# Softmax folded, low halves of 50 weight tiles made by adding transfers, q and k copies issued by ACT, and the conv norm's sums ordered ahead of q of heads 6 and 7

## The chip, the cores and the metric

The kernel runs on one core of a Trainium2 chip. The metric is the device time of one execution in microseconds (us). PE is the matmul engine, PEld its weight loads, DVE the vector engine, ACT the scalar engine, POOL GpSimd, and SP the engine that issues most transfers. Each engine does its instructions in the order in which they stand, and waits on semaphores for the others.

## The reference

Two blocks, one after the other, on 528 tokens (16 meta tokens and 512) of 1024 channels, all in float32. The change lies in the first:

```
n = rms(h); z = n @ w_in                       # q, k, v, glu, g_att, g_conv
s = (q * 64**-0.5) @ k, for 8 heads x 2 maps, chunk-causal mask
p = softmax(s);  a = p[0] - lam * p[1];  o = a @ v
y_att = rms(o) * 0.2;  u = glu_a * sigmoid(glu_b)
u = causal_dwconv(u, 31 taps);  u = silu(layernorm(u));  y_conv = u @ w_conv_out
m = sigmoid(g_att) * y_att + sigmoid(g_conv) * y_conv;  h = h + m @ w_out
h = h + ffn(h)                                 # gated, 2816 wide, 3-tap convs
```

The second block has two layers of a gated short conv and an 8-head retention.

## The kernel before

Every weight matrix is cut into tiles of 128x1024 float32 (512 KB), 300 of them, in the order of the list `order` (lines 78 to 121): 16 for the glu, then for each pair of heads two v tiles, and for each head a q, a k and a g_att tile, and for heads 0 to 4 a g_conv tile; then the rest of g_att and g_conv, w_conv_out, w_out, the FFN and the second block. Products are made to float32 precision from two float32r halves each: `proj` (line 150) does 24 matmuls, 8 of high weight with high x, 8 of low weight with high x, 8 of high weight with low x. So each weight tile must be split: `prep` (line 126) loads it to wraw, ACT casts it to the high half wh (line 138), and DVE subtracts to get the low half wl (line 139). Four tiles of each half are kept, so a tile's buffers come free when the tile four before it has been used.

The attention stage (lines 466 to 594) goes over 8 heads. Each head's q and k go from PSUM to qf (line 488), ql, kf and kl, and four transfers each copy them between the two halves of the partitions, to qh (line 493) and kk (line 506); POOL issues these. Then five query tiles t of scores s (PE), maximum mx (DVE), exp (ACT, with the scale 0.125 and the bias -0.125 mx), the difference a (DVE), its transposes tr (PE), their copy aTA or aTB (ACT), the products po with v, and pss, the sum of squares over a head. The PSUM tiles of the projections come from a pool of three (mmA, tag mm); tr, po and pss share one slot.

The conv of 31 taps (`conv`, lines 392 to 410: 240 DVE steps on line 405 and the running sum lnacc) is handed to the scheduler at head 5 with the lowest priority: it fills the room that DVE has left. The norm of the conv comes in two parts: `norm_1` (line 414) sums over channels (matmul lnm), subtracts the mean and adds up squares (acc_ln), and `norm_2` (line 424) sums those (matmul lnv), takes root and reciprocal (rs_ln) and applies silu. The call `later(steps, by)` (line 183) moves steps back in priority by so many. norm_1 stands in head 6 behind g_att with 300, norm_2 in head 7 with 0. The order of instructions on each engine is made by a scheduler from these priorities. After the heads come the products yc with w_conv_out, together with rb, which spreads the heads' scales, and then w_out (wo).

Of the kernel before, what the change touches and what calls it, by code (L numbers as in the profile page):

```python
# [13 lines left out]
AF = mybir.ActivationFunctionType  # L14
ALU = mybir.AluOpType
AX = mybir.AxisListType
# [3 lines left out]
D = 1024  # L20
# [18 lines left out]
N2, GCL, SP, LATE = 0, 0, 0, 2  # L39
CH, CB, N1, RB = 5, 20000, 300, 300  # L40
KB = 1
PSF = (4, 3, 1)
GC_EARLY = 5

PAR = {}
# [18 lines left out]
def kernel(ctx, tc, hT, par, pos, decay, w1, w2, out):  # L64
# [9 lines left out]
    def fv(ap):  # L74
        return ap.bitcast(F32)
# [50 lines left out]
    def prep():  # L126
        if state["next"] >= len(order):
            return
        src, idx = order[state["next"]]
        i = state["next"]  # L130
        state["next"] += 1
        src = src[idx]
        n = src.shape[1]
        raw = wpool.tile([P, D], F32, tag="wraw", bufs=2, name=f"wraw{i}")[:, :n]
        nc.sync.dma_start(raw, src)
        wl = wpool.tile([P, D], F32R, tag="wl", name=f"wl{i}")
        wh = wpool.tile([P, D], F32R, tag="wh", name=f"wh{i}")
        S.copy(wh[:, :n], raw)  # L138
        V.tensor_tensor(wl[:, :n], raw, fv(wh[:, :n]), ALU.subtract)  # L139
        ready.append((wh, wl))  # L140
# [272 lines left out]
    def norm_1():  # L413
        mu = npool.tile([P, T1], F32, tag="nrs", name="lnmu")
        for i, (c0, cn) in enumerate(C514):
            ps = mmA(f"lnm{i}")[:, :cn]
            PE.matmul(ps, lhsT=ones, rhs=ln["sum"][:, c0:c0 + cn], start=True, stop=True)
            S.activation(mu[:, c0:c0 + cn], ps, AF.Copy, scale=1.0 / D)
        ss = ln["ss"] = SumSq("ln")
        for k in range(NK):  # L420
            V.tensor_tensor(y[k], y[k], mu[:, :TQ], ALU.subtract)
            ss.add(y[k], 0, TQ)

    def norm_2():
        ss = ln["ss"]
        rs = npool.tile([P, T1], F32, tag="nrs", name="rs_ln")
        for i, (c0, cn) in enumerate(C514):
            ps = mmA(f"lnv{i}")[:, :cn]
            rstd(rs[:, c0:c0 + cn], ss.total(ps, c0, cn), D, epsc[:, 1:2])
        for k in range(NK):  # L430
            V.tensor_tensor(y[k], y[k], rs[:, :TQ], ALU.mult)
            S.activation(y[k], y[k], AF.Silu, bias=pc("conv_ln_b", k), scale=pc("conv_ln_w", k))
# [33 lines left out]
    for h in range(HEADS):  # L466
# [3 lines left out]
        if h % 2 == 0:  # L470
            wa, wb = getw(), getw()
            for tb in range(5):
                m = P if tb < 4 else META
                ps = mmA(f"v{h}_{tb}")[:m, :256]
                for p in range(3):
                    for k in range(NK):
                        w = (wa, wb)[k // 4][0 if p != 1 else 1][:, (k % 4) * 256:(k % 4 + 1) * 256]
                        x = (xh if p != 2 else xl)[k][:, tb * P:tb * P + m]
                        PE.matmul(ps, lhsT=x, rhs=w, start=p == 0 and k == 0, stop=p == 2 and k == NK - 1)  # L479
                S.copy(vt[(h // 2) % 2][:m, tb, :], ps)  # L480

        w = getw()
        qh = ap2.tile([P, 2, TQ + 2], F32R, tag="qh", bufs=1, name=f"qh{h}")
        for i, (c0, cn) in enumerate(C514):
            ps = mmA(f"q{h}_{i}")[:, :cn]
            proj(ps, w, xh, xl, TQ0 + c0, cn)
            c = slice(c0, c0 + cn)
            S.copy(qf[:, c], ps)
            for m in range(2):
                V.tensor_tensor(ql[MAP[m], m, c], ps[MAP[m]], fv(qf[MAP[m], c]), ALU.subtract)  # L490
        for m in range(2):
            for r in range(2):
                nc.gpsimd.dma_start(fv(qh[64 * r:64 * r + 64, m, :]), fv(qf[64 * m:64 * m + 64, :]))

# [9 lines left out]
        for m in range(2):  # L504
            for r in range(2):
                nc.gpsimd.dma_start(fv(kk[64 * r:64 * r + 64, m, :]), fv((kf, kl)[m ^ r][64 * m:64 * m + 64, :]))
        tg = None
# [4 lines left out]
        if h == HEADS - 1:  # L512
            att_rstd(("kf", "kl"))
            tg = g_att(h)
            later(norm_2, N2)
            for n in range(GC_EARLY, NK):
# [4 lines left out]
        if h == CH:  # L521
            later(conv, CB)
        if h == 6:
            later(norm_1, N1)
        v_ = vt[(h // 2) % 2]
# [3 lines left out]
        for t, (q0, qn, nkey) in enumerate(QT):  # L529
# [3 lines left out]
            if t < 4:  # L533
                ps = psS.tile([P, 2, 512], F32, tag="ps", name=f"s{h}_{t}")
                nw = nkey
                for m in range(2):
# [5 lines left out]
                    pm.append(ps[:qn, m, :nkey])  # L542
                V.tensor_reduce(mx[:qn], ps[:qn, :, :nkey], AX.X, ALU.max)
            else:
                for m in range(2):
# [5 lines left out]
                    pm.append(ps[:qn, 248:248 + T1])  # L551
                    V.tensor_reduce(mx[:qn, m:m + 1], pm[m], AX.X, ALU.max)
            V.tensor_scalar(mx[:qn], mx[:qn], -0.125, None, ALU.mult)
            sm = ap2.tile([P, 2], F32, tag="sm", name=f"sm{h}_{t}")
            pt = []
            for m in range(2):
                p_ = at[t] if m == 0 else ap2.tile([P, T1], F32, tag="p1", name=f"p1_{h}_{t}")
                S.activation(p_[:qn, :nkey], pm[m], AF.Exp, bias=mx[:qn, m:m + 1], scale=0.125,
                             accum_out=sm[:qn, m:m + 1])
                pt.append(p_)  # L560
# [511 lines left out]
```

## Time and profile before

| | us |
|---|---|
| three runs | 1880.42, 1882.37, 1882.59 |
| median | 1882.37 |
| the profiled execution | 1883.03 |
| its span, first to last instruction | 1881.2 |
| PE busy in the span | 1852.5 |
| DVE busy | 1311.3 |
| ACT busy | 836.1 |

Stages of the profiled execution: the glu to about 108 us, the heads to about 460, beside them yc from about 418 to 486, wo to 533, the FFN to about 900, then the second block. A busy PE is not a PE at its peak, since matmuls are pipelined and their ends are modelled; so matmuls are counted beside the busy time.

### The profile page before, as it was taken

The page shows a single profiled execution, that of the slowest core. Times are in us where ns is not written, and L with a number is a line of the kernel's source. Part 1 is how long each engine was busy: PE and PEld are TensorE (multiplying, and loading weights), DVE is VectorE, ACT ScalarE, POOL GpSimd, SP SyncE. Part 2 cuts the span into 40 slices and gives each one's busy share as a digit, 9 for nine tenths or more (in the row PEclk, how much of TensorE's full clock was granted, in tenths as well). Part 3 has the DMA queues.
Part 4 walks back from the last instruction along what each step waited for, and adds up shares of the span by engine and source line. Part 5 has one row for each costly group of instructions (what it writes and reads, how often), then busy time and mean ns, then how long its engine had stood idle before and what let it go on. Part 6 is the DMA issues. An engine that isn't in the chain of part 4 may idle for free.

```text
span 1881.2 us, 29256 instructions
## 1 busy us (share of the span) xinstructions
PE 1852.5 (98%) x11802; PEld 1685.7 (90%) x11802; DVE 1311.3 (70%) x2147; ACT 836.1 (44%) x1473; POOL 76.6 (4%) x123
## 2 busy tenths in 40 slices
PE   8999999999999999999999999999999999999997
PEld 7999999988999999988988888888899888888887
DVE  8999999876688777634588776454277877745424
ACT  7234455673445444433356553222355555422222
POOL 3000011000000000000000000000020000000000
PEclk9999999999999999999999999999999999999999
DMA  4332323222332222232323222222213222222221
GB/s 153 101 113 91 102 87 118 89 70 68 113 107 91 96 96 91 85 104 93 99 75 107 79 91 90 100 101 91 100 68 101 95 92 93 79 101 92 99 101 56
DMA packets 53047, 177.79 MB, mean 95 GB/s; under 512 B 6640, under 2 KB 10736, under 8 KB 52912
## 3 DMA queue, kind: packets, MB, share of 16 engines
q1 hardware_dynamic: 47696, 160.80, 24.8%
q0 software_dynamic: 5072, 15.12, 2.9%
q8 instruction: 93, 1.52, 0.3%
q14 instruction: 42, 0.34, 0.1%
q10 hardware_dynamic: 144, 0.00, 0.0%
HBM read 165.25 MB, written 2.10 MB: 89 GB/s over the span
## 4 chain that ended last, share of the span: by engine, by line
PE 96%; ACT 2%; DVE 1%; DMA 0%; issue 0%; POOL 0%; SPq 0%; DVEq 0%; ACTq 0%
PE up L157 13%; PE w L157 9%; PE dn L157 6%; PE rz L157 5%; PE cb L157 5%; PE cc L157 5%; PE cx L157 5%; PE cz L157 5%; PE rv L812 5%; PE rq L157 5%; PE rk L157 5%; PE v L479 3%; PE gc L157 3%; PE yc L157 3%; PE wo L157 2%; PE q L157 2%
## 5 line engine op out<-in xcount | busy, mean ns | idle before, releaser
L138 ACT CAST wh<-wraw 128x1024 fp32r<-128x1024 f32 (+1 forms) x300 | 313.3, 1045 | 490.3 <-PE dn L157 66.8
L139 DVE TENSOR_TENSOR wl<-wraw,wh 128x1024 fp32r<-128x1024 f32 (+1 forms) x300 | 364.4, 1215 | 189.2 <-ACT wh L138 188.6
L157 PE MATMUL up<-xhome,wh 128*128 128x258 f32 x1408 | 183.7, 283 | 0.0
L157 PEld LDWEIGHTS up<-xhome,wh 128*128 128x128 f32 x1408 | 175.3, 190 | 0.1
L405 DVE SCALAR_TENSOR_TENSOR y<-u,pr,y 128x514 f32<-128x514 f32 x240 | 170.2, 743 | 0.3
L157 PE MATMUL up<-xhome,wl 128*128 128x258 f32 x704 | 97.9, 281 | 0.0
L157 PEld LDWEIGHTS up<-xhome,wl 128*128 128x128 f32 x704 | 89.7, 189 | 0.0
L725 DVE SCALAR_TENSOR_TENSOR cv<-cg,pr,cv 128x256 f32<-128x256 f32 x176 | 83.7, 479 | 7.9 <-ACT cv L722 6.5
L722 ACT ACTIVATE cv<-cg,pr 128x256 f32<-128x256 f32 x88 | 52.7, 599 | 63.3 <-DVE cg L719 63.3
L812 PE MATMUL rv<-wh,xhome 128*128 128x256 f32 x512 | 75.5, 286 | 0.0
L157 PE MATMUL rq<-xhome,wh 128*128 128x512 f32 (+1 forms) x288 | 70.1, 373 | 1.3 <-ACT xhome L238 1.3
L812 PEld LDWEIGHTS rv<-wh,xhome 128*128 128x128 f32 x512 | 67.9, 191 | 1.7 <-issue 0.5
L157 PE MATMUL rk<-xhome,wh 128*128 128x512 f32 (+1 forms) x288 | 68.5, 368 | 0.0
L157 PE MATMUL rz<-xhome,wh 128*128 128x512 f32 x256 | 65.9, 391 | 0.0
L157 PE MATMUL w<-mh,wh 128*128 128x512 f32 (+1 forms) x320 | 65.7, 348 | 0.0
L157 PE MATMUL w<-mh,wl 128*128 128x512 f32 (+1 forms) x320 | 65.4, 347 | 0.0
L157 PE MATMUL cx<-xhome,wh 128*128 128x512 f32 x256 | 64.0, 390 | 0.0
L157 PE MATMUL cc<-xhome,wh 128*128 128x512 f32 x256 | 63.7, 390 | 0.0
L157 PE MATMUL cb<-xhome,wh 128*128 128x512 f32 x256 | 63.7, 389 | 0.0
L895 DVE RECIPROCAL rsq<-rsq 128x512 f32<-128x512 f32 x16 | 53.6, 3350 | 14.0 <-ACT rsq L894 14.0
L157 PE MATMUL cz<-xhome,wh 128*128 128x512 f32 x256 | 63.3, 389 | 0.0
L157 PE MATMUL w<-ml,wh 128*128 128x512 f32 (+1 forms) x300 | 62.4, 348 | 0.0
(379 smaller groups left out, 4000.1 us busy)
## 6 DMA issues: line engine op xcount, KB each, us to landing
wraw<-w_in SPq DMA_DIRECT2D x160, 512.0 KB, 3.2
wraw<-w_up SPq DMA_DIRECT2D x44, 512.0 KB, 3.2
wraw<-w_out SPq DMA_DIRECT2D x40, 512.0 KB, 3.2
wraw<-w_v SPq DMA_DIRECT2D x24, 512.0 KB, 3.2
wraw<-w_down SPq DMA_DIRECT2D x16, 512.0 KB, 3.2
qh<-qf POOLq DMA_DIRECT2D x32, 129.0 KB, 2.7
wraw<-w_conv_out SPq DMA_DIRECT2D x8, 512.0 KB, 3.2
dc<-dec POOLq DMA_DIRECT2D x16, 256.0 KB, 3.1
```

What stands on the lines that cost most here:

```text
L138: S.copy(wh[:, :n], raw)
L139: V.tensor_tensor(wl[:, :n], raw, fv(wh[:, :n]), ALU.subtract)
L157: PE.matmul(ps, lhsT=a[:, ks(k)], rhs=b[k][:, t0:t0 + n], start=first and i == 0, stop=last and i == len(steps) - 1)
L405: V.scalar_tensor_tensor(ys[i][:, :TQ], src, wj, ys[i][:, :TQ], ALU.mult, ALU.add)
L479: PE.matmul(ps, lhsT=x, rhs=w, start=p == 0 and k == 0, stop=p == 2 and k == NK - 1)
L722: S.activation(t, g[:, 0:256], AF.Identity, scale=pr[:, o:o + 1], bias=pc("ffn_dw_b", f))
L725: V.scalar_tensor_tensor(t, g[:, k:k + 256], pr[:, o:o + 1], t, ALU.mult, ALU.add)
L812: PE.matmul(ps, lhsT=xx, rhs=w, start=p == 0 and k == 0, stop=p == 2 and k == NK - 1)
L895: V.reciprocal(rr, rr)
```

## The change

Four parts.

1. Softmax: the scale 0.125 goes into the copy of q (qf and ql), the maximum is taken with its sign turned, and the multiplication of mx and the scale of exp go.
2. Low halves of weight tiles 6 to 55: in place of DVE's subtraction, ACT writes minus the rounded weight to wl, and POOL issues a transfer that reads the weight from memory again and adds it to wl where it lies.
3. The eight copies of q and k per head are issued by ACT in place of POOL.
4. norm_1 and norm_2 are called at the start of heads 6 and 7, ahead of q, with a priority raised by 300; the q matmuls of these heads are held behind the matmul of the sum just made.

```diff
@@ -37,10 +37,11 @@
 BY = (0, 0)
 LB = 0
 N2, GCL, SP, LATE = 0, 0, 0, 2
-CH, CB, N1, RB = 5, 20000, 300, 300
+CH, CB, N1, RB = 5, 20000, -300, 300
 KB = 1
 PSF = (4, 3, 1)
 GC_EARLY = 5
+ADDED = (6, 56)
 
 PAR = {}
 _off = 0
@@ -132,11 +133,18 @@
         src = src[idx]
         n = src.shape[1]
         raw = wpool.tile([P, D], F32, tag="wraw", bufs=2, name=f"wraw{i}")[:, :n]
-        nc.sync.dma_start(raw, src)
         wl = wpool.tile([P, D], F32R, tag="wl", name=f"wl{i}")
         wh = wpool.tile([P, D], F32R, tag="wh", name=f"wh{i}")
-        S.copy(wh[:, :n], raw)
-        V.tensor_tensor(wl[:, :n], raw, fv(wh[:, :n]), ALU.subtract)
+        if ADDED[0] <= i < ADDED[1]:
+
+            nc.sync.dma_start(raw, src)
+            S.copy(wh[:, :n], raw)
+            S.activation(wl[:, :n], raw, AF.Copy, scale=-1.0)
+            nc.gpsimd.dma_start(wl[:, :n], src, accum_op=ALU.add)
+        else:
+            nc.sync.dma_start(raw, src)
+            S.copy(wh[:, :n], raw)
+            V.tensor_tensor(wl[:, :n], raw, fv(wh[:, :n]), ALU.subtract)
         ready.append((wh, wl))
 
     def getw():
@@ -414,7 +422,7 @@
         mu = npool.tile([P, T1], F32, tag="nrs", name="lnmu")
         for i, (c0, cn) in enumerate(C514):
             ps = mmA(f"lnm{i}")[:, :cn]
-            PE.matmul(ps, lhsT=ones, rhs=ln["sum"][:, c0:c0 + cn], start=True, stop=True)
+            ln["mm"] = PE.matmul(ps, lhsT=ones, rhs=ln["sum"][:, c0:c0 + cn], start=True, stop=True)
             S.activation(mu[:, c0:c0 + cn], ps, AF.Copy, scale=1.0 / D)
         ss = ln["ss"] = SumSq("ln")
         for k in range(NK):
@@ -426,7 +434,8 @@
         rs = npool.tile([P, T1], F32, tag="nrs", name="rs_ln")
         for i, (c0, cn) in enumerate(C514):
             ps = mmA(f"lnv{i}")[:, :cn]
-            rstd(rs[:, c0:c0 + cn], ss.total(ps, c0, cn), D, epsc[:, 1:2])
+            ln["mm"] = PE.matmul(ps, lhsT=ones, rhs=ss.acc[:, c0:c0 + cn], start=True, stop=True)
+            rstd(rs[:, c0:c0 + cn], ps, D, epsc[:, 1:2])
         for k in range(NK):
             V.tensor_tensor(y[k], y[k], rs[:, :TQ], ALU.mult)
             S.activation(y[k], y[k], AF.Silu, bias=pc("conv_ln_b", k), scale=pc("conv_ln_w", k))
@@ -478,19 +487,24 @@
                         x = (xh if p != 2 else xl)[k][:, tb * P:tb * P + m]
                         PE.matmul(ps, lhsT=x, rhs=w, start=p == 0 and k == 0, stop=p == 2 and k == NK - 1)
                 S.copy(vt[(h // 2) % 2][:m, tb, :], ps)
+        if h == 6:
+            later(norm_1, N1)
+        if h == 6 + 1:
+            later(norm_2, N1)
 
         w = getw()
         qh = ap2.tile([P, 2, TQ + 2], F32R, tag="qh", bufs=1, name=f"qh{h}")
         for i, (c0, cn) in enumerate(C514):
             ps = mmA(f"q{h}_{i}")[:, :cn]
-            proj(ps, w, xh, xl, TQ0 + c0, cn)
+            with tc.issue_after(ln["mm"].ins) if h in (6, 6 + 1) else ExitStack():
+                proj(ps, w, xh, xl, TQ0 + c0, cn)
             c = slice(c0, c0 + cn)
-            S.copy(qf[:, c], ps)
+            S.activation(qf[:, c], ps, AF.Copy, scale=0.125)
             for m in range(2):
-                V.tensor_tensor(ql[MAP[m], m, c], ps[MAP[m]], fv(qf[MAP[m], c]), ALU.subtract)
+                V.scalar_tensor_tensor(ql[MAP[m], m, c], ps[MAP[m]], 0.125, fv(qf[MAP[m], c]), ALU.mult, ALU.subtract)
         for m in range(2):
             for r in range(2):
-                nc.gpsimd.dma_start(fv(qh[64 * r:64 * r + 64, m, :]), fv(qf[64 * m:64 * m + 64, :]))
+                nc.scalar.dma_start(fv(qh[64 * r:64 * r + 64, m, :]), fv(qf[64 * m:64 * m + 64, :]))
 
         w = getw()
         kk = ap2.tile([P, 2, T1], F32R, tag="kk", bufs=KB, name=f"kk{h}")
@@ -503,7 +517,7 @@
             split(ps, kf[:, c], kl[:, c])
         for m in range(2):
             for r in range(2):
-                nc.gpsimd.dma_start(fv(kk[64 * r:64 * r + 64, m, :]), fv((kf, kl)[m ^ r][64 * m:64 * m + 64, :]))
+                nc.scalar.dma_start(fv(kk[64 * r:64 * r + 64, m, :]), fv((kf, kl)[m ^ r][64 * m:64 * m + 64, :]))
         tg = None
         if h < HEADS - 1:
             tg = g_att(h)
@@ -512,7 +526,6 @@
         if h == HEADS - 1:
             att_rstd(("kf", "kl"))
             tg = g_att(h)
-            later(norm_2, N2)
             for n in range(GC_EARLY, NK):
                 later(lambda: g_conv(n), GCL)
             rs7 = npool.tile([P, T1], F32, tag="nrs", name="rs7")[:, :TQ]
@@ -520,8 +533,6 @@
             later(lambda: [split(y[k], uh[k][:, :TQ], ul[k][:, :TQ]) for k in range(NK)], SP)
         if h == CH:
             later(conv, CB)
-        if h == 6:
-            later(norm_1, N1)
         v_ = vt[(h // 2) % 2]
         aTA = ap2.tile([P, 2, 194], F32, tag="aTA", name=f"aTA{h}")
         aTB = ap2.tile([P, 5, 320], F32, tag="aTB", name=f"aTB{h}")
@@ -540,7 +551,7 @@
                     PE.matmul(ps[:qn, m, nkey - 64:nkey], lhsT=hid, rhs=negrow, start=False, stop=False)
                     PE.matmul(ps[:qn, m, :nw], lhsT=ql[:, m, q0:q0 + qn], rhs=kk[:, m, :nw], start=False, stop=True)
                     pm.append(ps[:qn, m, :nkey])
-                V.tensor_reduce(mx[:qn], ps[:qn, :, :nkey], AX.X, ALU.max)
+                V.tensor_reduce(mx[:qn], ps[:qn, :, :nkey], AX.X, ALU.max, negate=True)
             else:
                 for m in range(2):
                     ps = psS.tile([P, 1024], F32, tag="ps", name=f"s{h}_{t}_{m}")
@@ -549,13 +560,12 @@
                         PE.matmul(ps[:66, o:o + cn], lhsT=qh[:, m, q0:q0 + 66], rhs=kk[:, m, c0:c0 + cn], start=True, stop=False)
                         PE.matmul(ps[:66, o:o + cn], lhsT=ql[:, m, q0:q0 + 66], rhs=kk[:, m, c0:c0 + cn], start=False, stop=True)
                     pm.append(ps[:qn, 248:248 + T1])
-                    V.tensor_reduce(mx[:qn, m:m + 1], pm[m], AX.X, ALU.max)
-            V.tensor_scalar(mx[:qn], mx[:qn], -0.125, None, ALU.mult)
+                    V.tensor_reduce(mx[:qn, m:m + 1], pm[m], AX.X, ALU.max, negate=True)
             sm = ap2.tile([P, 2], F32, tag="sm", name=f"sm{h}_{t}")
             pt = []
             for m in range(2):
                 p_ = at[t] if m == 0 else ap2.tile([P, T1], F32, tag="p1", name=f"p1_{h}_{t}")
-                S.activation(p_[:qn, :nkey], pm[m], AF.Exp, bias=mx[:qn, m:m + 1], scale=0.125,
+                S.activation(p_[:qn, :nkey], pm[m], AF.Exp, bias=mx[:qn, m:m + 1],
                              accum_out=sm[:qn, m:m + 1])
                 pt.append(p_)
             V.reciprocal(sm[:qn], sm[:qn])
```

The matmuls are the same 11,696 of the program's order, and SP's list of loads is the same. From wo on, the orders of all engines are the same but for numbers. The order moves in three places that matter.

The first is PE where lnv stands, the sum of squares of the conv's norm (ga is g_att, gc g_conv, s scores, po and pss the end of a head). Before:

```order
L587 MATMUL pss_0_4313<-osq_0_4310,ones 128x194
L157 MATMUL ga_1_5016<-xhome,wh_4607 128x256 x4
L210 MATMUL lnv_5043<-acc_ln,ones 128x258
L580 MATMUL po_194_4316<-aTB_4187,v_1292 128x320 x3
L580 MATMUL po_194_4316<-aTB_4187,v_1292 128x192
L580 MATMUL po_194_4316<-aTB_4187,v_1292 128x64
L210 MATMUL lnv_5047<-acc_ln,ones 128x256
L157 MATMUL gc_0_5074<-xhome,wh_4846 128x258 x8
L157 MATMUL gc_0_5074<-xhome,wl_4845 128x258 x8
L157 MATMUL gc_0_5074<-xhome,wh_4846 128x258 x8
```

After:

```order
L165 MATMUL ga_1_4692<-xhome,wh_4349 128x256 x2
L437 MATMUL lnv_4856<-acc_ln,ones 128x258
L165 MATMUL ga_1_4692<-xhome,wh_4349 128x256 x6
L165 MATMUL ga_1_4692<-xhome,wl_4348 128x256 x8
L165 MATMUL ga_1_4692<-xhome,wh_4349 128x256 x4
L579 MATMUL tr_3_4285<-ident,a_1330 128x128 x4
L165 MATMUL ga_1_4692<-xhome,wh_4349 128x256 x3
L437 MATMUL lnv_4860<-acc_ln,ones 128x256
L165 MATMUL ga_1_4692<-xhome,wh_4349 128x256
L548 MATMUL s_0_4721<-kk_4597,qh_4529 66x80
```

The two lnv matmuls moved from g_att of head 7, where po and the next projection followed at once, into g_att of head 6, with 18 matmuls of g_att, a tr group of 4 and 3 more of g_att between the two.

The second is PE at the transposes tr of head 7, beside the products yc. Before:

```order
L615 MATMUL rb_1_5541<-rstd_sl_3186,sel 128x256
L569 MATMUL tr_0_5281<-ident,a_1311 128x66
L569 MATMUL tr_1_5302<-ident,a_1313 128x128 x2
L569 MATMUL tr_2_5324<-ident,a_1315 128x128 x3
L569 MATMUL tr_3_5347<-ident,a_1317 128x128 x4
L157 MATMUL yc_0_5552<-xhome,wh_5188 128x258 x8
L157 MATMUL yc_0_5552<-xhome,wl_5187 128x258 x8
L157 MATMUL yc_0_5552<-xhome,wh_5188 128x258 x8
L157 MATMUL yc_1_5578<-xhome,wh_5188 128x256 x2
L569 MATMUL tr_4_5375<-ident,a_1319 128x66 x5
L157 MATMUL yc_1_5578<-xhome,wh_5188 128x256 x6
```

After:

```order
L625 MATMUL rb_0_5478<-rstd_sl_3199,sel 128x258
L579 MATMUL tr_0_5295<-ident,a_1324 128x66
L625 MATMUL rb_1_5483<-rstd_sh_3198,sel 128x256
L625 MATMUL rb_1_5483<-rstd_sl_3199,sel 128x256
L165 MATMUL yc_0_5494<-xhome,wh_5143 128x258 x8
L165 MATMUL yc_0_5494<-xhome,wl_5142 128x258 x8
L165 MATMUL yc_0_5494<-xhome,wh_5143 128x258 x8
L165 MATMUL yc_1_5520<-xhome,wh_5143 128x256 x2
L579 MATMUL tr_1_5315<-ident,a_1326 128x128 x2
L165 MATMUL yc_1_5520<-xhome,wh_5143 128x256 x6
L165 MATMUL yc_1_5520<-xhome,wl_5142 128x256 x8
L165 MATMUL yc_1_5520<-xhome,wh_5143 128x256 x8
```

Four groups of tr that stood in one row are now apart, with a half of yc or more between each two.

The third is ACT behind the last q copy qf of head 4 (wh is the high half of a weight tile, wl the low one, aTA and aTB copies of transposes, tga the tanh of g_att). Before:

```order
L488 CAST qf<-q_1_3370 128x256
L138 CAST wh_3405<-wraw_3402 128x1024
L161 CAST kf_3409<-k_0_3411 128x256
L558 ACTIVATE a_1319,sm_4_3149<-s_4_0_3136,mx_4_3135 64x528
L558 ACTIVATE p_3_4_3151,sm_4_3149<-s_4_1_3142,mx_4_3135 64x528
L589 COPY ssq_1323<-pss_194_2788 1x320
L161 CAST kf_3409<-k_1_3438 128x272
L138 CAST wh_3472<-wraw_3469 128x1024
L572 COPY aTA_3043<-tr_0_3063 128x66
```

After:

```order
L502 ACTIVATE qf<-q_1_3386 128x256
L141 CAST wh_3420<-wraw_3418 128x1024
L507 DMA qh_3357<-qf 64x516 x3
L582 COPY aTA_3061<-tr_0_3080 128x66
L507 DMA qh_3357<-qf 64x516
L169 CAST kf_3426<-k_0_3428 128x256
L142 ACTIVATE wl_3487<-wraw_3486 128x1024
L169 CAST kf_3426<-k_1_3455 128x272
L141 CAST wh_3488<-wraw_3486 128x1024
L582 COPY aTA_3061<-tr_1_3100 128x2x128
L520 DMA kk_3425<-kf_3426 64x528
L520 DMA kk_3425<-kl_3427 64x528 x2
```

Among the copies that empty PSUM (qf, kf, aTA) now stand the wl copies and the issues of qh and kk. POOL's order has 50 issues of wl where the 64 issues of qh and kk were.

## Rows read from the trace of the kernel before

**Rows 1.** The page's first part: busy us (share of the span) xinstructions.

```profile
PE 1852.5 (98%) x11802; PEld 1685.7 (90%) x11802; DVE 1311.3 (70%) x2147; ACT 836.1 (44%) x1473; POOL 76.6 (4%) x123
```

**Rows 2.** Busy time by 50 us stretches, 300 to 450; the first line names the columns.

```profile
core 0: us, PE busy (x) PEld busy (x) DVE busy (x) ACT busy (x) POOL busy (x), PEclk, DMA share, GB/s
300.00:350.00 50.00, 50.00 (x412) 48.70 (x411) 46.49 (x91) 30.58 (x78) 4.07 (x8) 1.00 0.26 86
350.00:400.00 50.00, 47.01 (x347) 44.33 (x345) 38.30 (x76) 31.89 (x75) 8.16 (x16) 0.97 0.35 107
400.00:450.00 50.00, 46.99 (x348) 43.75 (x347) 31.59 (x65) 34.11 (x71) 0.00 (x0) 0.97 0.16 54
```

**Rows 3.** The same by 10 us stretches, same columns.

```profile
390.00:400.00 10.00, 8.24 (x47) 7.17 (x45) 8.74 (x12) 7.00 (x12) 0.97 (x2) 0.83 0.37 117
...
430.00:440.00 10.00, 8.55 (x65) 7.85 (x63) 5.56 (x12) 6.26 (x12) 0.00 (x0) 1.00 0.16 54
440.00:450.00 10.00, 9.16 (x63) 8.87 (x64) 5.58 (x10) 2.38 (x6) 0.00 (x0) 0.83 0.14 52
```

**Rows 4.** Waits of PE, 100 to 500 us: us in total, times, longest.

```profile
PE tr L569 <- ACT aTA L572: 1.7, 2, 1.3
PE po L580 <- ACT ssq L589: 1.2, 2, 0.6
PE lnv L210 <- ACT rs_ln L222: 1.2, 1, 1.2
PE yc L157 <- DVE tgc L607: 1.2, 1, 1.2
PE k L157 <- DVE ql L490: 1.1, 2, 0.7
PE gc L157 <- ACT rs_ln L222: 0.6, 1, 0.6
PE tr L569 <- ACT aTB L572: 0.6, 1, 0.6
```

**Rows 5.** PE in order of time: start us, us, operation, [idle before <-releaser].

```profile
362.77 1.08 PE L417 MATMUL lnm<-lnacc,ones 128*128 128x258 f32 x4
...
418.28 3.82 PE L157 MATMUL yc<-xhome,wh 128*128 128x258 f32 x15
```

**Rows 6.** Groups by line and shape, 50 to 400 us: busy, mean ns | idle before.

```profile
L405 DVE SCALAR_TENSOR_TENSOR y<-u,pr,y 128x514 f32<-128x514 f32 x237 | 168.2, 743 | 0.3
L139 DVE TENSOR_TENSOR wl<-wraw,wh 128x1024 fp32r<-128x1024 f32 x49 | 59.7, 1219 | 12.2 <-ACT wh L138 12.0
L138 ACT CAST wh<-wraw 128x1024 fp32r<-128x1024 f32 x48 | 50.3, 1048 | 16.2 <-PE gv L157 13.2 <-PE v L479 3.1
...
L493 POOL DMA_DIRECT2D qh<-qf x32 | 16.5, 526 | 320.4 <-ACT qf L488 136.6 <-issue 58.1 <-ACT p L563 32.9
```

**Rows 7.** DVE in order of time: last sum of conv, last sum of squares.

```profile
344.46 0.69 DVE L409 TENSOR_TENSOR lnacc<-lnacc,y 128x514 f32<-128x514 f32 x1
...
380.69 0.69 DVE L206 TENSOR_TENSOR acc_ln<-acc_ln,sq_ln 128x514 f32<-128x514 f32 x1
```

**Rows 8.** DMA issues on the page: KB each, median us to landing.

```profile
wraw<-w_in SPq DMA_DIRECT2D x160, 512.0 KB, 3.2
```

**Rows 9.** Issue instructions on SP and ACT: ns min/median/max, first and last start.

```profile
L135 SPq DMA_DIRECT2D wraw<-w_in x21: 327/328/332, 107.7 to 283.4; - x21
...
L166 ACTq DMA_DIRECT2D pr<-par x1: 442/442/442, 0.7 to 0.7; - x1
```

**Rows 10.** Table loads of ACT, 50 to 400 us, columns as in rows 6.

```profile
L222 ACT ACT_TABLE_LOAD x2 | 2.6, 1283 | 0.0
```

## The prediction

> **What bounds the kernel now.** I read the page's first part, then tables of stretches, then the waits of PE, then single instructions. The page [rows 1] shows PE busy 1852.5 us of 1881.2: all that any change of order can win is in the 28.7 us left, and in stretches where PE runs slowly without a gap. DVE has 70% and ACT 44% over the whole span, but this is an average over stages. The table of 50 us stretches [rows 2] shows the stage that the change touches: from 300 to 350 us PE has no gap (412 matmuls, so 0.121 us each) while DVE is busy 46.5 of 50; from 350 to 450 us PE loses 3.0 us in each stretch, and its granted clock has a mean of 0.97. The 10 us table [rows 3] finds the places: 390 to 400 and 430 to 450. In two of these stretches the clock has a mean of 0.83, which is a time at the lower level of 1.2 GHz: 0.17 of 10 us, so 1.7 us of work is lost each time, and both times PE had just stood idle. The waits of PE between 100 and 500 us [rows 4] name what it stood for, 7.6 us in all.
>
> I sort these losses into three. **A**, the norm of the conv: lnv 1.2, gc 0.6, one of the two po waits (0.6) and the longer k wait (0.7), 3.1 us, and the first clock loss, 1.7: **4.8 us**. **B**, the transposes of the last head: tr 1.7 and 0.6, the other po wait 0.6, 2.9 us, and the second clock loss, 1.7: **4.6 us**. **C**, yc for DVE, 1.2 us. A loss that no gap shows: the first 15 yc matmuls took 3.82 us [rows 5] where 15 x 0.121 is 1.8, so 2.0 us more. The ceiling is 7.6 + 3.4 + 2.0 = 13.0 us.
>
> Why A is there: the sum of the conv comes last of a long list on DVE. The 240 conv steps cost 743 ns each [rows 6], DVE does them in the room that the rest leaves, and the last sum starts at 344.46 us [rows 7]. Then lnm starts at 362.77 [rows 5], the squares are summed until 381.4 [rows 7], and lnv, which stands behind the last g_att on PE, meets a slot of PSUM that its own square root still holds.
>
> **The change, part by part.**
>
> *Low halves by adding transfers.* 50 DVE subtractions of 1219 ns go [rows 6]: 61 us of DVE work before 400 us. Nothing on PE waited for these directly; the gain is that the conv ends earlier, by up to 61 us, at about 284 us. In their place stand 50 ACT copies, which I cost like the 128x1024 cast beside them at 1048 ns [rows 6]: 52 us of ACT. Then come 50 POOL issues, for which the nearest row is the 526 ns of the q copies [rows 6], and 50 transfers that read the weight again, 512 KB each, for which the nearest row is 3.2 us to landing [rows 8]. No row shows a transfer that adds. I bound it from 3.2 us below to three times that, 9.6 us, above, and take 5. The tightest cover is the weight tile of g_att behind a pair of v tiles: its buffer comes free when v ends, and PE wants its low half 96 matmuls of q and k and 8 of its own later, 104 x 0.121 = 12.6 us. Three ACT copies (3.1), the issue (0.5) and 5 us make 8.7: hidden, cost 0. It would cost something from a landing of 9.0 us up, so the upper end costs 0.6 us at each of the four such places (heads 0, 2, 4 and 6), 2.4 us.
>
> *Copies of q and k issued by ACT.* 64 issues leave POOL, where they cost nobody anything, and come to ACT. The rows give 327 ns for an issue on SP and 442 for the only one on ACT [rows 9]: 21 to 28 us of ACT between 120 and 400 us. Each also makes ACT wait in its order, for DVE's kl or for the score matmuls that still read the old copy; behind it stand the copies that empty PSUM. POOL must be free of them, or they would stand behind adding transfers that wait for their copy. Together: 48 casts in 350 us [rows 6] are 6.9 per 50 us, so the new copies add 7.2; 64 issues over some 270 us add 3.9 to 5.2. ACT's 30.6 to 34.1 of 50 [rows 2] becomes 42 to 47, before the overlaps that busy time counts twice. This is the price of the change. Below, it is 0: ACT is under 100%, and with three PSUM tiles PE can be two groups of 24 matmuls (5.8 us) ahead. Above, each of the 16 groups of four issues holds PE for 1 us: 16. I take 2 us, near the lower end: ACT at 30.6 to 34.1 of 50 already stands beside a PE with no gap from 300 to 350.
>
> *Softmax folded.* 40 small DVE multiplications go, 32 subtractions take a scale as well, the scale moves to the q copy. All of it is DVE work in the stage where DVE gains room: 0.
>
> *The norm ordered earlier.* On PE, lnm now stands behind v of heads 6 and 7, before q of head 6, and lnv within g_att of head 6, before q of head 7. If conv ended late, PE would now be held in front of all of q; but conv ends some 50 us before, so that wait is 0. From lnm to the last sum took 18.6 us before [rows 5, 7]. Between them PE now has 130 large matmuls, 15.7 us, and about 2 us of small ones; DVE no longer has three subtractions of 1.2 us there, so I cost it 0, at most 2. The two square roots are now split by a tanh on ACT, which needs two more table loads of 1283 ns [rows 10]: 2.6 us of ACT, inside the sum above. The second lnv waits for a root that starts 25 matmuls (3 us) earlier. So A goes in full: **-4.8**.
>
> *The tail.* The transposes of head 7 stood in one row on PE, each waiting for the copy of the one before; now some 24 yc matmuls (2.9 us) stand between them. In that time ACT must do an exp, a table load, a root and the copy, about as much. I let 1.0 us of B stay: **-3.6**. C and the slow first yc stay; nothing there changed.
>
> Sum: -4.8 - 3.6 + 2.0 = -6.4 us. The profiled execution took 1883.03 us (span 1881.2 and 1.8 around it), 0.66 above the median of the three runs, 1882.37. So 1876.6 for a profiled run, **1876.0 us** against the median. Its own range is 1873 to 1880.
>
> **A rule against the change.** The 64 POOL issues before the change took a mean of 526 ns while DVE was 93% busy with the conv [rows 2, 6]; no stretched issue shows. The Trainium skill, in SBUF — State Buffer, section SBUF: two separate sides, warns of a "DVE blocks DMA" trap: a transfer issued on GpSimd can't get its descriptors written while DVE holds the shared ports in certain fast modes, and it names 620 ns that became 3100. By that figure each adding transfer would come about 2.5 us later, an estimate, which the 12.6 us would still cover. The trace speaks against it here, since the conv ran beside all those issues.
>
> **Rivals.**
>
> 1. *ACT becomes the bound* (slower). The place is q and k of every head: four issues in a row, 1.3 to 1.8 us, some of them waiting, ahead of the copies that empty PSUM. For it: ACT at up to 47 of 50 in its own order. Against it: PE had no gap beside ACT at 30.6. It decides from 0.53 us per group (8.4 / 16). At 0.8 us it costs 12.8: 1882.4 - 8.4 + 12.8 = 1886.8 us.
>
> 2. *The stall only moves.* The waits of A and B are of ACT's latency as much as of the conv's lateness: table loads and roots still stand between lnv and q, and between the last exps and tr. Then A is saved, B and its clock loss stay: -4.8 + 2 = -2.8, 1879.6 us. For it: ACT is fuller than before. Against it: the orders below the diff, where other matmuls stand in the gaps.
>
> 3. *Low halves come late.* As above, if a transfer that adds lands in 12 us or more: 3 us at each of four v pairs, 12 us, and a further clock loss: -6.4 + 12 + 1.7 = +7.3, 1889.7 us. Were it slower than a weight tile's pace, 48 tiles in 350 us or 7.3 us each, it would be tens of us more. For it: no row shows such a transfer, and the starved descriptors above would lengthen it. Against it: DMA is 0.16 to 0.35 busy [rows 2], so there is room for twice the bytes.
>
> That the change doesn't do what it says is excluded by the order of its instructions.
>
> **Chances.** The forecast's case 0.55, rival 1 0.17, rival 2 0.18, rival 3 0.10. A measurement of this kernel can tell about 0.2%, 3.8 us, so faster means under 1878.6 and slower over 1886.1. Forecast's case: 0.52 faster, 0.03 same. Rival 2: 0.06 faster, 0.11 same, 0.01 slower. Rival 1: 0.03, 0.05, 0.09. Rival 3: 0.02, 0.02, 0.06. Sum: 0.63 faster, 0.21 same, 0.16 slower. The range runs from the ceiling (1882.4 - 13.0 = 1869.4) to just past rival 1: 1869 to 1887; what is left out is rival 3's worse half and rival 1's.
>
> **What the profile after would show.** Right: the last conv step near 285 us, DVE under 40 of 50 from 300 on; PE with no lnv or gc wait, no clock below full around 390, tr waits under 1 us together; ACT 40 or more of 50 between 150 and 400; adding transfers landing in under 9 us. Wrong: PE waits for ACT (qf, kf, tga) spread over 130 to 380 us say rival 1; PE waits for DMA at the ninth matmul of a tile say rival 3; a tr wait and a clock of 0.83 near 440 again say rival 2.

## The result, and the profile after

The changed kernel takes 1898.59 us (median of four runs, 1896.26 to 1902.51) where the kernel before takes 1882.34: a ratio of 1.0094, interval 1.0078 to 1.011. It is slower by 16 us; the forecast was 6 us faster. The profiled execution took 1896.26 us, span 1894.3, so 13.1 us of span are to be accounted for.

The page of the changed kernel (first part; queues with packets, MB and share of 16 engines' span; issues with KB each and median us to landing):

```profile
PE 1856.1 (98%) x11802; PEld 1688.7 (89%) x11802; DVE 1254.9 (66%) x2057; ACT 887.7 (47%) x1525; POOL 87.1 (5%) x109
...
q1 hardware_dynamic: 47696, 160.80, 24.5%
q0 software_dynamic: 9200, 32.78, 8.9%
...
wl<-w_in POOLq DMA_DIRECT2D x42, 512.0 KB, 7.8
...
```

DVE has 56 us less work than before [rows 1], as it should, and ACT 52 more. What PE lost stands in the table of 50 us stretches, columns as in [rows 2]:

```profile
100.00:150.00 50.00, 47.31 (x398) 46.40 (x396) 44.93 (x89) 20.69 (x32) 6.05 (x7) 1.00 0.78 192
150.00:200.00 50.00, 47.00 (x367) 46.42 (x368) 42.52 (x86) 30.24 (x77) 4.32 (x5) 0.93 0.57 135
...
300.00:350.00 50.00, 47.48 (x389) 46.26 (x388) 20.68 (x44) 35.10 (x81) 5.18 (x6) 1.00 0.73 177
350.00:400.00 50.00, 46.69 (x350) 44.14 (x349) 28.03 (x53) 38.49 (x70) 4.32 (x5) 0.93 0.54 127
400.00:450.00 50.00, 48.85 (x369) 45.77 (x368) 26.35 (x57) 37.09 (x85) 1.73 (x2) 1.00 0.40 106
...
sum 400.00, PE 383.31 PEld 369.95 DVE 278.77 ACT 239.48 POOL 33.95; mean PE 47.91 PEld 46.24 DVE 34.85 ACT 29.93 POOL 4.24
```

The same eight stretches from 100 to 500 us of the kernel before:

```profile
sum 400.00, PE 392.34 PEld 379.66 DVE 342.01 ACT 207.44 POOL 35.03; mean PE 49.04 PEld 47.46 DVE 42.75 ACT 25.93 POOL 4.38
```

PE has 16.7 us of gaps in 400 where it had 7.7: 9.0 more. The clock is at a mean of 0.93 in two stretches (0.07 x 50 = 3.5 us each, 7.0), where it was at 0.97 in two (3.0): 4.0 more. Together 13.0 of the 13.1 us. By place, gaps and clock together (the stretches are of equal time, not of equal work: by 350 us the changed kernel is some 15 us behind):

| stretch, us | before | after | |
|---|---|---|---|
| 100 to 350 | 0.4 | 15.0 | +14.6, forecast at most +2.0, for ACT's issues |
| 350 to 400 (place A) | 4.5 | 6.8 | +2.3, forecast -4.8 |
| 400 to 500 (B and C) | 5.7 | 1.9 | -3.8, forecast -3.6 |

What PE waited for from 100 to 500 us, as in [rows 4]:

```profile
PE s L548 <- DMA kk<-kl: 5.0, 3, 2.4
PE s L548 <- DMA wraw<-w_in: 2.5, 1, 2.5
PE lnv L437 <- ACT rs_ln L230: 2.4, 1, 2.4
PE s L548 <- DMA wraw<-w_v: 1.7, 1, 1.7
PE s L548 <- DMA kk<-kf: 1.2, 1, 1.2
PE tr L579 <- ACT aTA L582: 1.2, 3, 0.7
PE tr L579 <- ACT ssq L599: 1.2, 2, 0.8
```

The first scores of a head (s) now wait for the copies of k and for DMA, 10.4 us in all, a wait that the kernel before doesn't have. A score reads no weight tile: where a weight load is named, a copy of k landed just behind it (in the first head the load at 148.8 us and the first copy of kl at 149.1, for a score that starts at 149.43). No row is a projection that waits for a low half. The adding transfers hurt, but not where they land: the transfers beside them come late. The issues between 100 and 400 us of the changed kernel (count, KB each, median us to landing):

```profile
q0 software_dynamic: 5376, 19.53, 36.7%
...
wl<-w_in POOLq DMA_DIRECT2D x30, 512.0 KB, 8.0
wraw<-w_in SPq DMA_DIRECT2D x30, 512.0 KB, 7.2
...
kk<-kf ACTq DMA_DIRECT2D x14, 132.0 KB, 6.1
kk<-kl ACTq DMA_DIRECT2D x14, 132.0 KB, 7.5
```

and of the kernel before:

```profile
q0 software_dynamic: 3072, 8.56, 10.8%
...
wraw<-w_in SPq DMA_DIRECT2D x30, 512.0 KB, 3.2
...
kk<-kf POOLq DMA_DIRECT2D x16, 132.0 KB, 2.9
kk<-kl POOLq DMA_DIRECT2D x16, 132.0 KB, 3.1
```

Every transfer shown takes twice as long or more: a weight load 7.2 us for 3.2, a copy of k 6.1 to 7.5 for 2.9 to 3.1. The first head shows how this reaches PE (in order of time: start us, us, operation, [idle before <-releaser]):

```profile
137.23 1.28 ACTq L520 DMA_DIRECT2D kk<-kf  x2
...
138.64 2.97 ACTq L520 DMA_DIRECT2D kk<-kl  x2
...
148.89 1.06 ACT L142 ACTIVATE wl<-wraw 128x1024 fp32r<-128x1024 f32 x1 [3.30 <-DMA wraw<-w_in]
...
149.43 0.23 PE L548 MATMUL s<-kk,qh 128*66 128x80 f32 x1 [2.46 <-DMA wraw<-w_in]
...
151.75 0.30 PE L548 MATMUL s<-kk,qh 128*66 128x80 f32 x1 [1.98 <-DMA kk<-kl]
```

The issue of two copies of kl holds ACT for 2.97 us; they land 10.5 and 11.4 us after their issues began, and PE waits twice for them. ACT's wl copy waits for a weight load, too. Then the clock falls. Ten-us stretches:

```profile
140.00:150.00 10.00, 7.32 (x62) 7.02 (x60) 7.34 (x12) 4.58 (x7) 0.86 (x1) 1.00 1.04 263
150.00:160.00 10.00, 8.25 (x50) 8.28 (x51) 5.76 (x13) 3.92 (x12) 0.86 (x1) 0.66 0.60 144
...
450.00:460.00 10.00, 9.33 (x77) 9.23 (x78) 9.58 (x18) 6.44 (x12) 0.00 (x0) 1.00 0.16 55
460.00:470.00 10.00, 10.00 (x87) 10.00 (x87) 5.88 (x12) 2.29 (x4) 0.00 (x0) 1.00 0.30 105
```

From 140 to 150 us the DMA engines have a share of 1.04: full by this measure, where the 50 us mean reads 0.78. The mean clock of 0.66 behind the two waits, part of the stretch at the 1.2 GHz level, is 0.34 x 10 = 3.4 us of work lost. The last two rows are place B, where the transposes of head 7 now stand (450.7 to 464.7 us): full clock, where before it was 0.83 [rows 3].

### The profile page after: what moved, and what is told of

Its sections match the earlier page's. It is cut to its first block, busy times and chain, and to the rows that moved or that the text cites. A ratio compares the mean times of both kernels' runs of the same rounds, so it can differ in the third digit from the quotient of the medians.

```text
span 1894.3 us, 29247 instructions
## 1 busy us (share of the span) xinstructions
PE 1856.1 (98%) x11802; PEld 1688.7 (89%) x11802; DVE 1254.9 (66%) x2057; ACT 887.7 (47%) x1525; POOL 87.1 (5%) x109
## 4 chain that ended last, share of the span: by engine, by line
PE 88%; DMA 4%; ACT 4%; DVE 3%; ACTq 1%; issue 1%; POOL 0%; SPq 0%; DVEq 0%
PE up L165 13%; PE w L165 9%; PE dn L165 6%; PE rz L165 5%; PE cb L165 5%; PE cc L165 5%; PE cx L165 5%; PE cz L165 5%; PE rv L822 5%; PE rq L165 5%; PE rk L165 4%; PE yc L165 3%; PE wo L165 2%; PE gv L165 2%; PE gg L165 2%; DMA wraw<-w_in 2%
## 5 line engine op out<-in xcount | busy, mean ns | idle before, releaser
L146 ACT CAST wh<-wraw 128x1024 fp32r<-128x1024 f32 (+1 forms) x250 | 260.9, 1045 | 469.9 <-PE dn L165 66.8
L147 DVE TENSOR_TENSOR wl<-wraw,wh 128x1024 fp32r<-128x1024 f32 (+1 forms) x250 | 303.5, 1215 | 177.6 <-ACT wh L146 177.1
L413 DVE SCALAR_TENSOR_TENSOR y<-u,pr,y 128x514 f32<-128x514 f32 x240 | 166.3, 745 | 1.2 <-ACT y L411 0.8
L142 ACT ACTIVATE wl<-wraw 128x1024 fp32r<-128x1024 f32 x50 | 52.6, 1059 | 38.2 <-DMA wraw<-w_in 13.9
```

Source lines behind the costliest of these rows:

```text
L142: S.activation(wl[:, :n], raw, AF.Copy, scale=-1.0)
L413: V.scalar_tensor_tensor(ys[i][:, :TQ], src, wj, ys[i][:, :TQ], ALU.mult, ALU.add)
```

## The experiments

Theory T: the adding transfers occupy the DMA engines, so copies of q and k come late. Theory A: ACT's order, with 64 issues in it, is the price. In the table S is the softmax fold, N the earlier norm, Q the copies issued by ACT (else by POOL), A the adding transfers with their tiles. The ratio is to the kernel before, whose median in these runs lay between 1880.9 and 1882.3.

| parts | run | us | ratio [interval] |
|---|---|---|---|
| S N Q A 6-55 (the change) | | 1898.6 | 1.0094 [1.0078, 1.011] |
| S N Q | e1 | 1875.6 | 0.9973 [0.9964, 0.9983] |
| S N A 6-55 | e2 | 1894.9 | 1.0078 [1.0063, 1.0093] |
| S Q A 6-55 | e3 | 1905.2 | 1.0129 [1.0113, 1.0146] |
| S A 6-55 | e4 | 1900.4 | 1.0108 [1.0093, 1.0123] |
| S N Q, plain transfers | e5 | 1876.9 | 0.9978 [0.9969, 0.9987] |
| S N | e6 | 1875.4 | 0.9969 [0.9958, 0.9981] |
| S Q | e7 | 1883.1 | 1.0014 [1.0005, 1.0023] |
| S N A 6-17 | e8 | 1873.3 | 0.9960 [0.9946, 0.9973] |
| S N A 18-29 | e9 | 1889.9 | 1.0042 [1.0028, 1.0056] |
| S N Q, two plain transfers | e10 | 1889.3 | 1.0047 [1.0031, 1.0062] |
| S | e11 | 1874.7 | 0.9964 [0.9952, 0.9977] |
| N | f1 | 1880.5 | 0.9995 [0.9986, 1.0004] |
| S, old chain length | f2 | 1880.9 | 1.0000 [0.9991, 1.0009] |
| S A 18-29 | f3 | 1881.3 | 1.0005 [0.9996, 1.0014] |
| S A 6-17 | f4 | 1876.3 | 0.9975 [0.9964, 0.9987] |

### e1: the change without adding transfers

```diff
-ADDED = (6, 56)
+ADDED = (0, 0)
```

> The change without its adding transfers: DVE subtracts all low halves as before; the softmax fold, the ACT-issued copies of q and k and the earlier norm stay. Theory T (the adding transfers keep the DMA engines busy; copies of q and k land late and their issue instructions on ACT stretch): the copies land in about 3 us instead of 5.4 to 7.1, no issue on ACT above 0.7 us, no score matmul waits for a copy, and the time is 1874 to 1881. Theory A (ACT's order, with the issues in it, is the price): the score waits stay and the time is above 1890.

Measured 1875.6. The copies of q land in 2.3 us, those of k in a median of 2.4, and no score waits for them. Theory T holds: the adding transfers cost 23 us, the rest of the change gains about 5 (3 to 7 by the interval). One of its numbers missed: a single issue on ACT still took up to 1.87 us. And PE waited 1.9 us at a g_att for ACT, behind issues of about 0.5 us each and a table load, with a low clock after it.

### e2, e3, e4: other parts away

```diff
-                nc.scalar.dma_start(fv(qh[64 * r:64 * r + 64, m, :]), fv(qf[64 * m:64 * m + 64, :]))
+                nc.gpsimd.dma_start(fv(qh[64 * r:64 * r + 64, m, :]), fv(qf[64 * m:64 * m + 64, :]))
...
-                nc.scalar.dma_start(fv(kk[64 * r:64 * r + 64, m, :]), fv((kf, kl)[m ^ r][64 * m:64 * m + 64, :]))
+                nc.gpsimd.dma_start(fv(kk[64 * r:64 * r + 64, m, :]), fv((kf, kl)[m ^ r][64 * m:64 * m + 64, :]))
```

That is e2. In e3 the issues stay with ACT, and norm_1 and norm_2 are called where they stood before, with N1 = 300 and without `issue_after`. e4 has both edits.

> The change with the copies of q and k issued by POOL again, the adding transfers and all else kept. Theory T: copies still land in 5 us or more, and stand on POOL behind adding transfers too, so the score waits stay: 1892 to 1905. Theory A: the score waits go and the time is 1876 to 1884.

> The change with the norm of the conv back in its old place and with no matmuls held for it; the rest kept. Both theories: the score waits between 130 and 350 us (some 11 us) stay; only 360 to 450 us can differ. If the earlier norm is worth the 4.8 us that were forecast for it, 1900 to 1904; if it costs (a wait of 2.4 us at lnv and a low clock behind it in the changed kernel), 1893 to 1897.

> The kernel before with the softmax fold and the adding transfers alone: copies by POOL, norm in its old place. Theory T: 8 to 16 us slower than before, 1890 to 1898, with copies landing in 5 us or more and scores waiting for them. Theory A: no slower than before, 1876 to 1884, since ACT issues nothing.

e2 took 1894.9, inside theory T's range, and e4 1900.4, just above T's; both are far above theory A's 1876 to 1884. e3, 1905.2, doesn't decide between the two, since both keep its score waits; it asks about the norm, and came out 1.2 us above the 1900 to 1904 of a norm that is worth 4.8. Whoever issues them, copies beside adding transfers land late: in e2, between 100 and 400 us, those of k had medians of 9.2 and 8.1 us. The Trainium skill, in DMA: Bandwidth & Descriptors, section Issuing engines are not separate DMA queues, says that transfers started by different engines run on the same 16 DMA engines and interleave there; these runs agree, with 9.2 us from POOL and 6.1 from ACT for the same copies, both at least twice the 2.9 of the kernel before; why POOL's are the later ones, no run shows.

e3 against the change says that with adding transfers the earlier norm is worth 6.6 us; e2 against e4 says 5.5.

### e5 and e10: is it the adding, or the time on the DMA engines?

e5 leaves out the addition:

```diff
-            nc.gpsimd.dma_start(wl[:, :n], src, accum_op=ALU.add)
+            nc.gpsimd.dma_start(wl[:, :n], src)
```

and e10 issues a second plain transfer behind each, to unused memory:

```diff
-            nc.gpsimd.dma_start(wl[:, :n], src)
+            first = nc.gpsimd.dma_start(wl[:, :n], src)
+            with tc.issue_after(first.ins):
+                nc.gpsimd.dma_start(w1["twin"][i], src)
...
+    w1["twin"] = nc.dram_tensor("twin", (60, P, D), F32, kind="Internal").ap()
```

> The change with the 50 transfers to the low halves as plain copies of the same bytes to the same place (the weight overwrites what ACT wrote, so the low half holds the whole weight: the addition is left out). All orders and waits stay. If the adding itself is what fills the DMA engines (a packet of it at a median of 328 ns against 159 ns for a load's): transfers land in 3 to 4.5 us, copies of q and k in 3 to 4, and the time is 1874 to 1884. If it is the second reading of 26 MB as such: copies stay above 5 us and the time above 1892.

> As the run with plain transfers (1876.9), and behind each a second plain transfer of the same bytes to unused memory, so that DMA engines are busy about as long as with the adding ones (2 packets at 159 ns against one at 328); the addition is left out here too. If it is the occupied time of the DMA engines that delays the copies: score waits come back, 1888 to 1902. If it is something of the adding itself (its order, its place behind the other packets): 1875 to 1881.

e5 took 1876.9 and e10 1889.3. Queue q0 on the pages of e1 (no such transfers), e5 and e10:

```profile
q0 software_dynamic: 2000, 6.56, 1.2%
```

```profile
q0 software_dynamic: 9200, 32.78, 5.9%
```

```profile
q0 software_dynamic: 10800, 59.00, 9.3%
```

A share times its span, less the 22.5 us of e1's queue, over 50: a plain transfer of 512 KB occupies the 16 engines for 1.76 us, two of them for 3.06, and an adding one, from the 8.9% shown further up, for 2.92. So the adding transfer moves the same bytes from memory and occupies the engines 1.66 times as long. The Trainium skill, in Collectives: The Full Stack, section The bandwidth ceiling: the fold count and why AG ≠ RS ≠ AR, says of a collective's adding phase, among four ranks on one chip, that it is slower because the add needs two source reads where a copy has one, and gives a measured ratio of 1.93; the direction agrees here, with 1.66.

With one plain transfer PE's waits for DMA are 0.9 us in all, with two they are back, though the addition is left out:

```profile
PE s L548 <- DMA kk<-kf: 0.9, 1, 0.9
```

```profile
PE s L550 <- DMA kk<-kl: 2.9, 3, 1.8
PE s L550 <- DMA wraw<-w_in: 2.0, 1, 2.0
PE s L550 <- DMA wraw<-w_v: 1.9, 1, 1.9
```

A second transfer, which occupies the engines about as long as the addition does (1.30 us against 1.16), thus brings back 12.4 of the 21.7 us between e5 and the change. It also takes POOL a second issue and writes to memory; no run parts these from the occupied time. The other 9.3 us stay open: the adding transfer's own issue takes POOL 863 ns for 527, and its landing 7.8 us in the median (tiles of w_in) where the first of the two plain ones takes 5.5, but no run tells apart which of this counts. An expectation missed as well: in e5 the copies of k still landed in 5.9 us in the median, not 3 to 4, and that cost next to nothing. They have slack: landings of up to 8.7 us cost PE the one wait of 0.9 us in e5, landings of up to 11.4 the 10.4 us of the change. From 140 to 150 us the DMA share is 0.94 in e5, where PE has no gap, and 1.01 in e10, where it is busy 7.95 of 10.

### e6, e7, e11, f1: which part gains?

Each is the kernel before with some of the parts, by the edits of the change.

> The kernel before with the softmax fold and the earlier norm alone: DVE subtracts, POOL issues the copies. The run without adding transfers took 1875.6 and showed a wait of 1.9 us at g_att for ACT, behind issues of copies, with a low clock after it (3.6 us together). If ACT's issues are to blame, that wait goes: 1870 to 1874. If they are worth something, 1876 to 1882.

> The kernel before with the softmax fold and the copies issued by ACT alone. If moving the issues is free or costs a few us: 1880 to 1887. If it brings the gain of the run without adding transfers, 1874 to 1878, and the earlier norm then brings nothing.

> The kernel before with the softmax fold alone: no adding, copies by POOL, norm in its old place. If the 5.6 us of the run with softmax fold and earlier norm come from the norm: 1879 to 1884. If from the softmax: 1874 to 1877.

> The kernel before with the earlier norm alone, without the softmax fold. If the earlier norm by itself takes away the waits at lnv, as the prediction had it: 1874 to 1878. If the gain of 5.6 to 6.6 us belongs to the softmax fold alone: 1880 to 1884.

e6 (S N) 1875.4, e7 (S Q) 1883.1, e11 (S alone) 1874.7, f1 (N alone) 1880.5. So the softmax fold, which the prediction put at 0, by itself brings as much as the whole change without adding transfers, and the earlier norm, which was to bring 4.8, brings none by itself or beside the fold. Beside fold and ACT's issues, though, it is worth 7.5 (e1 against e7). The stretches of e11 that hold A and B, and the one before them:

```profile
300.00:350.00 50.00, 48.32 (x383) 46.06 (x382) 47.68 (x89) 30.89 (x79) 4.09 (x8) 1.00 0.26 79
350.00:400.00 50.00, 50.00 (x403) 48.79 (x402) 34.05 (x62) 32.37 (x72) 8.19 (x16) 1.00 0.39 114
400.00:450.00 50.00, 48.94 (x381) 46.37 (x380) 36.85 (x73) 33.96 (x69) 0.00 (x0) 1.00 0.19 64
```

403 and 381 matmuls where 347 and 348 were, and 383 in the stretch before, where 412 were [rows 2]: 60 more in all. In f1 the waits of lnv, gc and tr are gone, as forecast, and others have come, so that PE has 8.3 us of gaps from 100 to 500 us where it had 7.7:

```profile
PE s L548 <- ACT p L569: 3.1, 1, 3.1
PE pss L598 <- DVE og L595: 2.8, 1, 2.8
```

ACT's issues cost 8.4 us beside the fold alone (e7 against e11), and 0.2 beside fold and earlier norm (e1 against e6). e6's expectation of a gain without those issues missed: the wait at g_att of e1 went, others came.

### f2: why does the fold gain?

Against e11:

```diff
                     V.tensor_reduce(mx[:qn, m:m + 1], pm[m], AX.X, ALU.max, negate=True)
+            V.tensor_scalar(mx[:qn], mx[:qn], 1.0, None, ALU.mult)
```

> The run with the softmax fold alone, with a DVE multiplication by 1.0 put back between the maximum and the exp, where the old one stood: the same number of DVE operations and the old order on PE, the scale still folded. If the gain comes from the chain being one operation shorter and from the order that the scheduler makes of it: the gain goes, 1880 to 1884. If from the exp or the copies being cheaper: it stays, 1873 to 1877.

1880.9, the time of the kernel before. The order on PE is then, row by row, that of the kernel before too, and so are PE's seven waits of [rows 4], each to 0.1 us; none of them is a score that waits for mx or p. f2 puts back the operation and the order at once; that the time hangs on the order is read from these waits. With the chain from maximum to exp one DVE operation shorter, the scheduler makes another order. In e11's, the two lnv stand together and a tr group behind them:

```
L437 MATMUL lnv_5008<-acc_ln,ones 128x258
L437 MATMUL lnv_5012<-acc_ln,ones 128x256
L577 MATMUL tr_0_4690<-ident,a_1311 128x66
L165 MATMUL gc_0_5039<-xhome,wh_4810 128x258 x8
```

and the tr groups of head 7 stand apart, with yc between, as in the order of the change. The fold isn't the only way there, nor a sure one. With the earlier norm and no fold (f1) the groups stand apart too, from 440.2 to 453.9 us; with the fold and ACT's issues (e7) four of them are in one row again, with waits like the old ones. One group of f1, then one of e7:

```profile
444.07 0.38 PE L580 MATMUL tr<-ident,a 128*128 128x128 f32 x2
```

```profile
439.78 0.44 PE L577 MATMUL tr<-ident,a 128*128 128x128 f32 x2 [1.36 <-ACT aTA L580]
```

So the piece of order that the prediction read correctly hangs on no single part of the change.

### e8, e9, f3, f4: twelve adding transfers, at two places

Against e6 (e8, e9) and e11 (f3, f4); here for e8 and f4:

```diff
-ADDED = (0, 0)
+ADDED = (6, 18)
```

e8 and f4 have tiles 6 to 17, whose transfers go out before any copy of q; e9 and f3 have 18 to 29, beside the first copies. e8 and e9 have the earlier norm, f3 and f4 the old one.

> The run with softmax fold and earlier norm, with adding transfers for weight tiles 6 to 17 alone, which land before the first copies of q are issued (some 130 us). If only the meeting of adding transfers and copies costs, DVE's 12 subtractions less (14.6 us, conv ends earlier) come free: no slower than the run without them, by 0 to 4 us faster. If adding transfers cost wherever they stand, 4 to 5 us slower (12 of 50 of the 19.5 that all of them cost).

> As the run with 12 adding transfers in the glu (1873.3), but for weight tiles 18 to 29, whose transfers go out between about 107 and 200 us, beside the first copies of q and k; as many transfers, and DVE is spared as much. If the meeting with the copies is the price: score waits between 140 and 200 us and 4 to 10 us slower than the glu's 12, 1877 to 1883. If the place does not matter: 1872 to 1875.

> As the run with 12 adding transfers beside the first copies (1889.9), with the norm in its old place. That run lost some 8 us between 125 and 200 us and some 6 near 388, where the norm's silu stood ahead of the exps of head 7. If both are costs of the adding transfers: 1887 to 1891. If the second belongs to the earlier norm: 1881 to 1885, and the transfers' own price for 12 is about 8.

> The softmax fold and adding transfers for weight tiles 6 to 17 alone, the norm in its old place. Softmax fold alone took 1874.7, and with the earlier norm and these 12 transfers 1873.3. If the 12 transfers bring a gain of their own: 1871 to 1874; if none: 1874 to 1876.

In the glu they cost nothing that these intervals can tell (e8 1873.3 against 1875.4 without, f4 1876.3 against 1874.7), and bring nothing either, though DVE is spared 12 subtractions. Beside the copies the same number costs 6.6 us with the old norm (f3 against e11) and 14.5 with the earlier one (e9 against e6). f3's first scores show the place:

```profile
150.37 0.30 PE L546 MATMUL s<-kk,qh 128*66 128x80 f32 x1 [4.96 <-issue]
```

with copies of k landing in up to 11.5 us; that wait, and the 2.6 us lost to the low clock behind it (a mean of 0.74 from 150 to 160 us), cover the 6.6. e9 has such a wait as well, and near 388 us, long after its last adding transfer, two more. There the silu of the norm holds ACT ahead of the exps of head 7:

```profile
PE s L548 <- ACT p L568: 3.3, 1, 3.3
...
PE po L590 <- ACT aTB L582: 1.2, 1, 1.2
```

f3 hasn't these two; e6, with the earlier norm and no adding transfers, hasn't them either. By these runs the second loss needs both.

e1, e6, e8, e11 and f4 are faster than both kernels, by 0.25 to 0.4% than the one before; which of them is best, the intervals leave open.

## Why the prediction was wrong

**Low halves by adding transfers: the step that failed.** The prediction priced them by their own landing against the 12.6 us until PE wants the low half. That held: PE never waited for one, and their landings lie inside the 3.2 to 9.6 us bounded but for the tail (shortest, median and longest):

```profile
DMA to landing us min/median/max: 5.1/7.4/11.6
```

What was not priced is the time that they take from other transfers. "DMA is 0.16 to 0.35 busy, so there is room for twice the bytes" took the mean of 50 us for the moment, and bytes for time: an adding transfer occupies the engines for 2.92 us where a plain one of the same bytes takes 1.76, and from 140 to 150 us the share was 1.04. The landing of the copies of k, 3.0 us before, is in no term of the prediction, yet these are the transfers that PE came to stand for. The term was 0; measured beside the rest of the change it is 23 us (the change against e1). Rival 3 had the right resource and the wrong victim, and with 10 in 100 and 1889.7 it was too small.

**Softmax folded: 0 forecast, -6.6 measured.** It was judged by DVE time. The operation that went stood in the chain on which the scheduler builds its order, and the gain comes and goes with that order (f2).

**The norm ordered earlier: -4.8 forecast, 0 measured by itself** (f1) and beside the fold (e6 against e11). By itself it takes away the waits it was to take away, of lnv and gc, and the term failed in letting no others come: PE then stands 3.1 us at a score and 2.8 at pss. Nor is it one number: it gains 7.5 us beside ACT's issues (e1 against e7) and 5.5 to 6.6 beside all adding transfers, and costs 8.6 beside twelve of them (e9 against f3). In the changed kernel the lnv wait is even longer, 2.4 us for 1.2 [rows 4], behind an issue of kk that held ACT for 2.8 us and a table load of 1.3; the condition that the prediction named (conv ends by about 284 us) was met, the last sum of the conv starting at 283.6, and decided nothing: in e6 the last sum starts at 341.5 and PE has no lnv wait.

**The tail: -3.6 forecast, -3.8 measured** in 400 to 500 us. The waits for transposes of head 7, all but 0.8 us, and the low clock behind them went for the reason given, other matmuls between the groups. That the sum fits so well is in part luck: C's 1.2 us, forecast to stay, went too, and 1.0 us of other waits came.

**Copies issued by ACT: +2 forecast; 0.2 or 8.4 measured** without adding transfers (e1 against e6, e7 against e11) and 3.7 or 4.8 beside them (the change against e2, e3 against e4), by the order beside them. The bounds of 0 and 16 held. ACT was forecast at 42 to 47 of 50 and came to 38.5 at most.

The sum of the other parts, 1876.0 forecast, was 1875.6 (e1). That is luck: a sum that came out right over terms that didn't. The gain that the fold has by itself stood at 0, and the 4.8 of the norm, nothing by itself, is 7.5 beside fold and ACT's issues.

## What to carry to other kernels

Price a new transfer by what it does to the transfers around it: list those that PE waits for soon (here copies of q and k, landing in 3 us before; in the first head of e11 the last issue starts at 135.9 and the scores at 144.9, so it may land in up to 9.0 us), and read the DMA share in stretches as short as such a transfer's slack. A transfer that adds is not a copy. Where a scheduler sets the order, undo the parts of a change one at a time, and in pairs, before crediting a gain to the part that seems to aim at it: one small operation in a chain moved the time by 6 us.

## What the runs showed of the hardware

An adding transfer of 512 KB occupied the 16 DMA engines 2.92 us against 1.76 for a plain one, and its issue took POOL 863 ns against 527. An issue instruction on ACT isn't of a fixed length: 468 ns at the least, up to 2.83 us for one while the DMA engines were full (a share of 1.07 from 380 to 384 us), and ACT's next instruction stood 2.40 us idle behind that one:

```profile
L520 ACTq DMA_DIRECT2D kk<-kf x16: 468/587/2827, 137.2 to 418.5; - x16
```

In e1, with no adding transfers, the longest issue was still 1.87 us; what lengthened that one was not tried.
